# Streaming the high and low parts of an activation in one 512-column matmul, in a two-block transformer kernel

## The chip, the cores and the metric

The kernel runs on one core of a Trainium2 chip. The metric is the device time of one execution in microseconds (us); less is better. The time before is the median of three runs.

## The reference

Two transformer layers are computed one after the other in float32 on x of 256 tokens by 2048 features. Nearly all the arithmetic is in products with large weights:

```python
# first block
u = rms_norm(x); hq, hf, hi, hg, aq, ak, av = split(u @ w_in)        # 2048 x 7168
h = x + rms_norm(concat(hgrn2(hq, hf, hi, hg), dilated_attn(aq, ak, av)) @ w_out)
up = conv3(rms_norm(h) @ w_up); gate, val = split(up)                # 2048 x 11264
h = h + rms_norm((gelu(gate) * val) @ w_down)                        # 5632 x 2048
h = h + (p @ w_pe) * sigmoid(h @ w_pg)
# second block
q, k, v, u, vg = split(rms_norm(h) @ w_in_2)                         # 2048 x 5120
h = h + concat(diff_attn(q, k, v), gmlp(gelu(u), gelu(vg))) @ w_out_2
f = rms_norm(h)
h = h + (silu(f @ w1_2) * (f @ w3_2)) @ w2_2                         # 2048 x 11264, 5632 x 2048
h = h + (p_2 @ pl_w_up_2) * sigmoid(h @ pl_w_gate_2)
out = rms_norm(h)
```

## The kernel before

Every product with a weight is computed as three products of reduced-precision parts. An operand `a` is split into a high part (a cast to the type fp32r) and a low part (`a` less its high part), and `w*a` becomes `whi*ahi + whi*alo + wlo*ahi`.

The weights are streamed in **units** of 512 KB (256 rows of the contraction by 512 columns, 128 partitions of 4 KB): `load` (line 148) issues the transfer on SP's queue into one of three `raw` buffers, `split` (line 155) makes the high part on ScalarE (line 163) and the low part on VectorE (line 164), each with four buffers. `run` (line 166) walks through all 856 units in the order in which the phases have listed them: it issues the load of unit i+5, the split of unit i+3, the matmuls of unit i, then the unit's `post` if it is the last of its group, and then one `tick`. A tick advances each of the side tasks (generators) by one piece; norms, attention heads and evictions are such tasks. So the order of instructions on every engine is written out here, in units, and engines work through their queues in order.

`group` (line 194) lists the units of one **group**, 512 output columns. It accumulates in one tile of PSUM of 1024 columns (two banks), and there are two such tiles. Form "A" has the activation stationary and 512 columns of the weight moving. Form "B" (lines 231 to 243) has a 128x128 piece of the weight stationary and 256 tokens moving: per unit 4 column blocks x 2 contraction tiles x 3 matmuls,

```python
for q, (w_, m_) in enumerate(((hi, ah), (hi, al), (lo, ah))):
    self.mm(ps[:, n * T:(n + 1) * T], w_[:, b, n * P:(n + 1) * P], m_, s, lst and b == 1 and q == 2)
```

With `first` the contraction tile is the outer loop, so that a group can start before all its tiles are there. All matmuls come from line 192.

After a group's last unit its epilogue evicts PSUM: `scaled` (line 279) multiplies each bank by the reciprocal norm on VectorE (line 282); `gate_ep` (line 952) takes a sigmoid on ScalarE; `post_norm` (line 763) squares on ScalarE and scales on VectorE; `residual_ep` (line 1247) adds to h on VectorE (line 1252). High and low parts of the activations are in separate tiles `bh`, `bl` (lines 117 and 118; two pairs) and `hid` (line 880), and are made by `part_hi` (ScalarE, lines 294 and 296) and `part_lo` (VectorE, lines 300 and 302).

After a product whose norm is added to h, `post_finish` (line 793) makes the tiles for the next product pair by pair: multiply on POOL (line 809), add on VectorE (line 813), high part, low part, in a pipeline of 11 stages of which the later ones are issued one per tick (line 821). The next product's units are issued between them. What follows needs the new norm only at its eviction: w_up's first epilogue waits for the flag "r3" (line 893), w_in_2's first for "r6" (line 1001), ffn's first for "r8" (line 1300).

Of the 856 units, 776 are of form B and 80 (parts of w_in and w_in_2) of form A. Groups 0 and 1 of w_out and w_out_2 visit their contraction tiles out of order; the last group of pl_w_gate_2 (line 207) is done in three pieces.

Of the kernel before, what the change touches and what calls it, by code (L numbers as in the profile page):

```python
# [16 lines left out]
P = 128  # L17
T = 256
# [9 lines left out]
# columns of the per-feature constants, [128, n] each  # L28
# [15 lines left out]
class Unit:  # L44
    """512 KB of a weight: 256 rows of the contraction by 512 columns."""
# [5 lines left out]
class Kernel:  # L51
# [55 lines left out]
    def setup(self):  # L107
# [27 lines left out]
    def side(self, name, n=512, count=1):  # L135
        """Banks for side products, once as many have been read: done() tells so."""
# [57 lines left out]
    def group(self, name, w, g, form, acts, kus, epilogue, first=None, part=(True, True), hold=None, tail=None):  # L194
        """Units of one group of 512 columns; acts() gives per kt the (hi, lo) moving or stationary operand.
        epilogue(ps) is called, as a task, after the last of them."""
# [3 lines left out]
        def mk(j, ku):  # L200
            def pe(hi, lo):
# [5 lines left out]
                if tail:  # L207
                    # three pieces one after the other over the last two units
# [7 lines left out]
                    for i, (piece, ns) in enumerate(zip(st["pc"], ((0, 1), (2,), (3,)))):  # L216
                        if j == nk - 2 and i:
                            break
                        for ku_, hi_, lo_ in kept if i and late else kept[-1:]:
                            for q_, n in enumerate(ns):  # L220
                                for b in range(2):
                                    ah, al = acts(2 * ku_ + b)
# [6 lines left out]
                    if j < nk - 2:  # L229
                        kept.clear()  # L230
                elif form == "B":
# [4 lines left out]
                    for n, b in order:  # L236
                        ah, al = acts(2 * ku + b)
# [6 lines left out]
                else:  # L244
# [4 lines left out]
                    for t, b in order:  # L249
                        ah, al = acts(2 * ku + b)  # L250
# [19 lines left out]
    def rstd(self, ss, n, name, out=None):  # L270
        """1/sqrt(ss/D + eps) of sums of squares in PSUM."""
# [7 lines left out]
    def scaled(self, ps, dst, rbc, nb=2):  # L279
        """dst[:, 4, T] = ps * rbc, bank by bank."""  # L280
# [24 lines left out]
    def pair_stages(self, out, gain):  # L305
        """hi and lo of two tiles of h (times a gain), apart."""
# [15 lines left out]
    def start(self):  # L322
# [5 lines left out]
        # matmuls on nothing open the tensor engine's clock gate while the first loads are on their way  # L328
# [28 lines left out]
    def first(self, c, go=False):  # L357
        """Chunk c of x: its load, then its two parts and its squares."""
# [8 lines left out]
        bh, bl = self.buf[0]  # L367
# [425 lines left out]
    def post_finish(self, name, sqs, out, gain, nxt):  # L793
# [23 lines left out]
        for s in range(11):  # L817
# [3 lines left out]
            if s > 4 or s % 2:  # L821
                yield 0
# [705 lines left out]
```

## Time and profile before

| | |
|---|---|
| Median of three runs | 2604.04 us (2603.99 to 2606.28) |
| Span of the profiled execution | 2603.7 us |
| TensorE busy | 2574.3 us, 20346 matmuls and as many weight loads |
| VectorE busy | 1546.5 us |
| ScalarE busy | 1191.4 us |
| POOL (GpSimd) busy | 370.9 us |
| Mean granted TensorE clock | 0.995 of full speed |
| DMA | 469.22 MB, mean 180 GB/s |

The profiled execution's own time is its span of 2603.7 us from first to last instruction; the runs' times are 0.3 us above it. Matmuls are pipelined and the profile models their ends, so the time of one is read from the distance between starts. PE is TensorE, PEld its weight loads, DVE VectorE, ACT ScalarE, POOL GpSimd and SP the engine whose queue issues transfers.

### The profile page before, as it was taken

What the parts mean: (1) busy time and instruction counts of PE and PEld (TensorE: products, weight loads), DVE (VectorE), ACT (ScalarE), POOL (GpSimd) and SP (SyncE); (2) the same over time, 40 slices, a digit from 0 to 9 for tenths busy, and PEclk for the clock granted to TensorE, in tenths of its full rate; (3) what the DMA queues carried; (4) which work ended last, traced back from release to release, by engine and by line L of the source; (5) the groups of instructions that cost most, each with busy time, mean ns of one, the idle gap of its engine ahead of it and who ended that gap; (6) DMA issues with size and microseconds to landing.
All of it is one profiled execution on the core that took longest, in us unless ns stands there. A gap on an engine that the chain in (4) does not pass through costs nothing.

```text
span 2603.7 us, 48034 instructions
## 1 busy us (share of the span) xinstructions
PE 2574.3 (99%) x20346; PEld 2523.0 (97%) x20346; DVE 1546.5 (59%) x1619; ACT 1191.4 (46%) x1497; POOL 370.9 (14%) x299
## 2 busy tenths in 40 slices
PE   8999999999999999999999999999999999999998
PEld 7999999999999999999999899999999999999998
DVE  7568885677666666444565575565555555444445
ACT  5554544465544455333455444444444344333344
POOL 5214442220000000000221030010000000000012
PEclk9999999999999999999999999999999999999999
DMA  6554335555555555555555544455555555555554
GB/s 231 190 171 138 131 129 199 181 185 194 183 183 186 181 184 184 185 186 180 193 191 173 202 170 170 161 180 186 181 184 179 187 186 181 184 183 182 186 205 144
DMA packets 129817, 469.22 MB, mean 180 GB/s; under 512 B 14528, under 2 KB 15824, under 8 KB 129344
## 3 DMA queue, kind: packets, MB, share of 16 engines
q1 hardware_dynamic: 127488, 457.17, 51.4%
q0 software_dynamic: 1968, 8.96, 1.0%
q8 instruction: 159, 2.61, 0.4%
q14 instruction: 58, 0.48, 0.1%
q10 hardware_dynamic: 144, 0.01, 0.0%
HBM read 461.10 MB, written 4.98 MB: 179 GB/s over the span
## 4 chain that ended last, share of the span: by engine, by line
PE 97%; DVE 1%; issue 0%; DMA 0%; ACT 0%; DVEq 0%; SPq 0%; ACTq 0%
PE ps_w_in L192 20%; PE ps_w_up L192 20%; PE ps_ffn L192 19%; PE ps_w L192 10%; PE ps_w_down L192 10%; PE ps_w_out L192 7%; PE ps_w_pg L192 4%; PE ps_pl_gate L192 3%; PE sc L192 1%; PE d L192 1%; DVE wlo L164 1%; PE tl L192 0%; DVE bl L302 0%; DMA raw<-w_in 0%; DVE h L813 0%
## 5 line engine op out<-in xcount | busy, mean ns | idle before, releaser
L164 DVE TENSOR_TENSOR wlo<-raw,whi 128x1024 fp32r<-128x1024 f32 x856 | 1119.7, 1311 | 970.8 <-ACT whi L163 967.9
L163 ACT CAST whi<-raw 128x1024 fp32r<-128x1024 f32 x856 | 893.2, 1046 | 1031.3 <-PE ps_ffn L192 220.1
L192 PE MATMUL ps_w_up<-bl,whi 128*128 128x256 f32 x1408 | 400.3, 284 | 3.5 <-DVE bl L302 3.5
L192 PE MATMUL ps_w_up<-bh,whi 128*128 128x256 f32 x1408 | 400.2, 284 | 0.0
L192 PE MATMUL ps_w_up<-bh,wlo 128*128 128x256 f32 x1408 | 400.1, 284 | 0.0
L192 PE MATMUL ps_ffn<-bh,whi 128*128 128x256 f32 x1408 | 399.1, 283 | 0.0
L192 PE MATMUL ps_ffn<-bl,whi 128*128 128x256 f32 x1408 | 399.0, 283 | 0.0
L192 PE MATMUL ps_ffn<-bh,wlo 128*128 128x256 f32 x1408 | 399.0, 283 | 0.0
L192 PEld LDWEIGHTS ps_w_up<-bl,whi 128*128 128x128 f32 x1408 | 271.8, 193 | 3.7 <-DVE bl L302 3.7
L192 PEld LDWEIGHTS ps_w_up<-bh,whi 128*128 128x128 f32 x1408 | 271.8, 193 | 0.0
L192 PEld LDWEIGHTS ps_w_up<-bh,wlo 128*128 128x128 f32 x1408 | 271.8, 193 | 0.0
L192 PEld LDWEIGHTS ps_ffn<-bl,whi 128*128 128x128 f32 x1408 | 270.6, 192 | 0.0
L192 PEld LDWEIGHTS ps_ffn<-bh,whi 128*128 128x128 f32 x1408 | 270.6, 192 | 0.0
L192 PEld LDWEIGHTS ps_ffn<-bh,wlo 128*128 128x128 f32 x1408 | 270.6, 192 | 0.0
L192 PE MATMUL ps_w_in<-bh,whi 128*128 128x256 f32 x896 | 256.8, 287 | 0.0
L192 PE MATMUL ps_w_in<-bh,wlo 128*128 128x256 f32 x896 | 253.9, 283 | 1.1 <-DVE wlo L164 1.1
L192 PE MATMUL ps_w_in<-bl,whi 128*128 128x256 f32 x896 | 253.7, 283 | 0.0
L192 PEld LDWEIGHTS ps_w_in<-bh,wlo 128*128 128x128 f32 x896 | 171.8, 192 | 1.5 <-DVE wlo L164 1.5
L192 PEld LDWEIGHTS ps_w_in<-bh,whi 128*128 128x128 f32 x896 | 171.8, 192 | 0.7 <-ACT whi L163 0.2
L192 PEld LDWEIGHTS ps_w_in<-bl,whi 128*128 128x128 f32 x896 | 171.9, 192 | 0.5
L192 PE MATMUL ps_w_out<-bh,wlo 128*128 128x256 f32 x512 | 145.1, 283 | 1.4 <-DVE wlo L164 1.4
L192 PE MATMUL ps_w_out<-bh,whi 128*128 128x256 f32 x512 | 146.1, 285 | 0.0
(330 smaller groups left out, 5281.0 us busy)
## 6 DMA issues: line engine op xcount, KB each, us to landing
raw<-ffn_w SPq DMA_DIRECT2D x264, 512.0 KB, 4.3
raw<-w_in SPq DMA_DIRECT2D x192, 512.0 KB, 3.3
raw<-w_up SPq DMA_DIRECT2D x176, 512.0 KB, 3.3
raw<-w_down SPq DMA_DIRECT2D x88, 512.0 KB, 3.3
raw<-w_out SPq DMA_DIRECT2D x64, 512.0 KB, 3.3
raw<-w_pg SPq DMA_DIRECT2D x32, 512.0 KB, 3.4
raw<-pl_w_gate SPq DMA_DIRECT2D x32, 512.0 KB, 4.4
x<-xT SPq DMA_DIRECT2D x8, 256.0 KB, 4.4
```

Of the source, the lines that this page charges most:

```text
L163: nc.scalar.copy(out=hf, in_=u.raw)
L164: nc.vector.tensor_tensor(out=lf, in0=u.raw, in1=hf.bitcast(F32), op=ALU.subtract)
L192: self.nc.tensor.matmul(out, lhsT, rhs, start=start, stop=stop, skip_group_check=True)
```

## The change

A new form "C" takes the place of form B for w_up, ffn_w13_2, w_down, ffn_w2_2, w_pg, for the parts of w_in and w_in_2 that were of form B, for columns 1024 and up of w_out and w_out_2, and for columns up to 1536 of pl_w_gate_2. The high and low part of a contraction tile lie side by side in one tile, so that both are 512 neighbouring columns. A unit is still 512 KB, but of 512 rows of the contraction by 256 columns, and a group has 256 output columns. The high part of the weight streams both parts of the activation in one matmul of 512 columns into one bank of PSUM; the low part streams the high part of the activation into the second half of that bank. At the eviction the two halves are added.

```diff
-            h = self.bp.tile([P, KT, T], F32R, name=f"bh{i}", tag=f"bh{i}")
-            l = self.bp.tile([P, KT, T], F32R, name=f"bl{i}", tag=f"bl{i}")
-            self.buf.append((h, l))
+            t = self.bp.tile([P, KT, 2, T], F32R, name=f"bhl{i}", tag=f"bhl{i}")
+            self.buf.append((t[:, :, 0, :], t[:, :, 1, :], t))
...
+                elif form == "C":
+                    hi, lo = (x.rearrange("p a b -> p (a b)").rearrange("p (b n) -> p b n", b=4) for x in (hi, lo))
+                    order = [(n, b) for n in range(2) for b in range(4)]
+                    if first:
+                        order = [(n, b) for b in range(4) for n in range(2)]
+                    for n, b in order:
+                        ah, _, both = acts(4 * ku + b)
+                        cs = slice(n * P, (n + 1) * P)
+                        self.mm(ps[:, n * 512:(n + 1) * 512], hi[:, b, cs], both.rearrange("p a t -> p (a t)"),
+                                fst and b == 0, False)
+                        self.mm(ps[:, n * 512 + T:(n + 1) * 512], lo[:, b, cs], ah, False, lst and b == 3)
...
+    def parts(self, ps):
+        v = ps.rearrange("p (n x t) -> p n x t", n=2, x=2)
+        return v[:, :, 0, :], v[:, :, 1, :]
+
+    def join(self, ps, dst):
+        x, y = self.parts(ps)
+        self.nc.scalar.copy(out=dst, in_=y)
+        self.nc.vector.tensor_tensor(out=dst, in0=x, in1=dst, op=ALU.add)
+        return dst
+
+    def scaled2(self, ps, dst, rbc):
+        self.scale2(self.join(ps, dst), dst, rbc)
+
+    def scale2(self, t, dst, rbc):
+        self.nc.vector.tensor_tensor(out=dst, in0=t, in1=rbc.unsqueeze(1).to_broadcast([P, 2, T]), op=ALU.mult)
```

The epilogues of C groups use these. `post_norm` joins into y, squares that on ScalarE and scales it in place; `gate_ep` joins, then takes the sigmoid; `residual_ep` adds both halves to h one after the other:

```diff
+            if half is not None:
+                k = 4 * g + 2 * half
+                for v in self.parts(ps):
+                    self.nc.vector.tensor_tensor(out=self.h[:, k:k + 2, :], in0=v, in1=self.h[:, k:k + 2, :],
+                                                 op=ALU.add)
```

In `post_finish` the stages are issued at a closer spacing, and w_up's and ffn's epilogues empty PSUM before they wait for the norm; for that the tiles that they write (`z`) are made earlier, with two memsets on POOL in `enter2`:

```diff
-            if s > 4 or s % 2:
+            if s % 2 or s == 10:
                 yield 0
...
-                if j == 0:
-                    yield from self.until("r3")
+                if j > 1:
+                    yield from self.until(f"cv{j - 2}")
+                z = self.z[j % 2]
+                d = z[:, 2 * half:2 * half + 2, 2:]
+                self.join(ps, d)
+                yield from self.until("r3")
+                if j == 0 and half == 0:
                     self.new_hid("hid", 1)
...
+                self.scale2(d, d, self.rbc)
+                if not half:
+                    return
```

In w_in_2 the first epilogue still waits for "r6" before it reads PSUM. The host lays the weights out for the new units.

## Rows read from the trace of the kernel before

**Rows 1.** The page: span, and TensorE's busy time, share and instructions.

```profile
span 2603.7 us, 48034 instructions
PE 2574.3 (99%) x20346; PEld 2523.0 (97%) x20346; DVE 1546.5 (59%) x1619; ACT 1191.4 (46%) x1497; POOL 370.9 (14%) x299
```

**Rows 2.** The page: the chain that ended last, shares of the span by line.

```profile
PE ps_w_in L192 20%; PE ps_w_up L192 20%; PE ps_ffn L192 19%; PE ps_w L192 10%; PE ps_w_down L192 10%; PE ps_w_out L192 7%; PE ps_w_pg L192 4%; PE ps_pl_gate L192 3%; PE sc L192 1%; PE d L192 1%; DVE wlo L164 1%; PE tl L192 0%; DVE bl L302 0%; DMA raw<-w_in 0%; DVE h L813 0%
```

**Rows 3.** TensorE's waits, longest first: us in total, times, longest us.

```profile
PE ps_w_pg L192 <- DVE bl L300: 3.7, 1, 3.7
```

**Rows 4.** The chain in order of time: start us, us, what, matmuls.

```profile
180.64 2.72 PE ps_w_in L192 x12
...
553.36 472.30 PE ps_w_up L192 x3936
```

**Rows 5.** Groups by form, VectorE and ScalarE: busy us, mean ns | idle before.

```profile
L164 DVE TENSOR_TENSOR wlo<-raw,whi 128x1024 fp32r<-128x1024 f32 x856 | 1119.7, 1311 | 970.8 <-ACT whi L163 967.9 <-PE ps_w_in L192 1.2
...
L282 DVE TENSOR_TENSOR z<-ps_w_up,rbc 128x512 f32<-128x512 f32 x44 | 28.3, 686 | 13.9 <-PE ps_w_up L192 13.9
...
L163 ACT CAST whi<-raw 128x1024 fp32r<-128x1024 f32 x856 | 893.2, 1046 | 1031.3 <-PE ps_ffn L192 220.1 <-PE ps_w L192 145.9 <-PE ps_w_down L192 141.2
...
L861 ACT COPY plu<-ps_pl_up 128x512 f32<-128x512 f32 x8 | 4.3, 588 | 1.9 <-PE ps_pl_up L192 1.9
```

**Rows 6.** Stretches: busy us of each engine, granted clock, DMA share, GB/s.

```profile
170.00:400.00 230.00, 228.96 (x1559) 211.73 (x1559) 187.73 (x224) 104.01 (x178) 98.45 (x83) 1.00 0.40 138
...
560.00:1025.00 465.00, 465.00 (x3877) 465.00 (x3876) 319.30 (x389) 235.50 (x288) 28.19 (x21) 1.00 0.53 184
```

**Rows 7.** ScalarE's waits: us in total, times, longest us.

```profile
ACT whi L163 <- PE ps_ffn L192: 220.1, 127, 1.8
...
ACT whi L163 <- DMA raw<-w_in: 56.7, 33, 5.1
```

**Rows 8.** Transfers of w_up: KB each, median us from issue to landing.

```profile
raw<-w_up SPq DMA_DIRECT2D x176, 512.0 KB, 3.3
```

**Rows 9.** Timeline of VectorE at w_up's beginning: start us, us, instructions.

```profile
519.39 0.87 DVE L302 SCALAR_TENSOR_TENSOR bl<-h,cst,bh 128x256 fp32r<-128x256 f32 x2
...
520.79 0.87 DVE L302 SCALAR_TENSOR_TENSOR bl<-h,cst,bh 128x256 fp32r<-128x256 f32 x2
521.58 1.21 DVE L164 TENSOR_TENSOR wlo<-raw,whi 128x1024 fp32r<-128x1024 f32 x1
...
523.32 0.87 DVE L302 SCALAR_TENSOR_TENSOR bl<-h,cst,bh 128x256 fp32r<-128x256 f32 x2
```

**Rows 10.** The chain in order of time, beginnings of w_up and w_pg.

```profile
515.29 37.21 PE ps_w_up L192 x287
...
1297.03 31.40 PE ps_w_pg L192 x239
```

**Rows 11.** Timeline of VectorE at w_pg's beginning.

```profile
1300.80 0.68 DVE L300 TENSOR_TENSOR bl<-h,bh 128x512 fp32r<-128x512 f32 x1
...
1302.00 0.68 DVE L300 TENSOR_TENSOR bl<-h,bh 128x512 fp32r<-128x512 f32 x1
```

**Rows 12.** Timeline of ScalarE in w_in_2: first and last of the statistics' eight instructions.

```profile
1415.56 1.28 ACT L275 ACT_TABLE_LOAD   x1
...
1421.95 0.20 ACT L276 ACTIVATE rcol<-rcol 128x2 f32<-128x2 f32 x1
```

**Rows 13.** TensorE's waits from 1390 to 1440 us.

```profile
PE ps_w_in L192 <- DVE wlo L164: 1.1, 2, 0.8
```

**Rows 14.** Timeline of TensorE at w_up's beginning.

```profile
515.29 0.58 PE L192 MATMUL ps_w_up<-bl,whi 128*128 128x256 f32 x1 [3.46 <-DVE bl L302]
...
516.10 0.42 PE L192 MATMUL ps_w_up<-bl,whi 128*128 128x256 f32 x1
516.31 0.41 PE L192 MATMUL ps_w_up<-bh,wlo 128*128 128x256 f32 x1
...
521.00 0.29 PE L192 MATMUL ps_w_up<-bh,whi 128*128 128x256 f32 x1
```

More of the change, by code (lines that the diff above doesn't have):

```diff
@@ L366, in first @@
             return
[L367 removed]
+        bh, bl, _ = self.buf[0]
         xc = self.xc.pop(c)
@@ L729, in enter2 @@
         self.ple("p2T")
+        self.zp = self.push("conv", side="right")
+        self.z = []
+        for i in range(2):
+            z = self.zp.tile([P, 4, T + 2], F32, name=f"z{i}", tag=f"z{i}")
+            nc.gpsimd.memset(z[:, :, 0:2], 0.0)
+            self.z.append(z)
     def ple(self, name):
@@ L765, in post_norm, with ep @@
         sqs = []
-        def ep(g):
+        def ep(g, half=None):
             def f(ps):
                 nc = self.nc
-                if g == 0:
+                if g == 0 and not half:
                     self.yp = self.push(f"y{name}", side="right")
@@ L921, in phase3 @@
         for j in range(FT // 2):
-            self.group("w_up", "w_up", j, "B", acts, range(8), ep(j), first=j == 0)
+            for half in range(2):
+                self.group("w_up", "w_up", 2 * j + half, "C", acts, range(4), ep(j, half), first=j + half == 0)
     def phase4(self):
@@ L930, in ep0 @@
             self.ple("pT")
-            return ep(0)(ps)
-        for g in range(4):
-            self.group("w_down", "w_down", g, "B", self.hid, range(FT // 2), ep(g) if g else ep0)
+            return ep(0, 0)(ps)
+        for g in range(8):
+            self.group("w_down", "w_down", g, "C", self.hid, range(FT // 4), ep(g // 2, g % 2) if g else ep0)
         def ep_pe(g):
@@ L964, in gate_ep @@
         for f in stages:
-            for b in range(2):
-                f(2 * g + b)
+            f(g)
             yield 0
@@ L1245, in diff_head, with residual_ep @@
         self.flags.update((f"mixb{2 * h}", f"mixb{2 * h + 1}"))
-    def residual_ep(self, g, out, gain, flag):
+    def residual_ep(self, g, out, gain, flag, half=None):
         def f(ps):
+            if half is not None:
+                k = 4 * g + 2 * half
+                for v in self.parts(ps):
+                    self.nc.vector.tensor_tensor(out=self.h[:, k:k + 2, :], in0=v, in1=self.h[:, k:k + 2, :],
+                                                 op=ALU.add)
+                for s in (*self.pair_stages(out, gain), *((self.sq_stage,) if flag else ())):
+                    s(2 * g + half)
+                yield 0
+                if g == 3 and half and flag:
+                    yield from self.rest(2)
+                    yield from self.stats(flag)
+                return
             for b in range(2):
@@ L1279, in ep0 @@
             self.pop("p6a")
+            self.zp = self.push("glu", side="right")
+            self.z = {}
             self.new_acc("acc7")
@@ L1309, in f @@
                 self.hid_pair(j, z[:, 0:2, :])
+                self.flags.add(f"gl{j}")
             return f
         for j in range(FT // 2):
-            self.group("ffn", "ffn_w13_2", j, "B", acts, range(8), ep(j))
+            for half in range(2):
+                self.group("ffn", "ffn_w13_2", 2 * j + half, "C", acts, range(4), ep(j, half))
     def phase9(self):
@@ L1354, in ep @@
             return f
-        for g in range(4):
-            self.group("pl_gate", "pl_w_gate_2", g, "B", acts, range(8), ep(g),
-                       tail=self.last_piece if g == 3 else None)
+        for g in range(6):
+            self.group("pl_gatec", "pl_w_gate_2c", g, "C", acts, range(4), ep(g))
+        self.group("pl_gate", "pl_w_gate_2", 0, "B", acts, range(8), ep(6), tail=self.last_piece)
     def last_piece(self, i, ps):
```

263 lines of the change are left out of this document (154 added, 109 removed).

## Prediction

> **What bounds the kernel now.** I read the page first: TensorE is busy for 2574.3 us of a span of 2603.7 us [rows 1], and the chain that ended last is made of matmuls of line 192, weight by weight, with nothing else over 1% [rows 2]. So time comes off only where TensorE issues less, or where it stops waiting. It waits little: its longest stop between units is 3.7 us [rows 3]. That leaves the price of a matmul. Durations of single matmuls overlap, so the pitch is read from the chain in order of time: 3936 matmuls of 256 columns took 472.30 us, 120.0 ns each; 12 matmuls of 512 columns (the form in which the weight is the moving operand) took 2.72 us, 226.7 ns each [rows 4]. 512 columns cost 13.3 ns less than twice 256 columns: a matmul has a fixed part of about that size, and the change removes fixed parts.
>
> **What it removes.** In a unit of form B each of the 8 (column block, contraction tile) pairs issues three 256-column matmuls: 24 x 120.0 ns = 2.880 us. In form C the first two become one of 512 columns: 8 x (226.7 + 120.0) = 2.773 us. Form C takes 352 units of w_up and ffn_w13_2 (88 groups of 4), 176 of w_down and ffn_w2_2 (16 groups of 11), 64 of w_in, 48 of w_in_2, 32 of the two w_out, 32 of w_pg and 24 of pl_w_gate_2: 728 of 856, in 154 groups. So 5824 matmuls go, and as many weight loads: 5824 x 13.3 ns = **77.7 us**. The 80 units of form A and the 48 left in form B stay as they are. No row shows a 512-column matmul right after a 256-column one. Its bounds are 226.7 ns and 240.0 ns, twice the short one [rows 4]. I take 226.7: that row has the same width, type and engine, and at a pitch of 120 ns a weight load of the same size already hides beneath each short matmul, so it does beneath a long one.
>
> The Trainium skill ("TensorE: Matmul & The Clock Gate", section Back-to-back issue gap) gives the gap as the columns at 2.4 GHz plus 2.5 ns. By it a fused pair would save 2.5 ns and the whole change 14.6 us; the rows show a fixed part five times as long and decide here, but the rule returns among the rivals.
>
> **What it adds beside TensorE.** The halves of a C group lie side by side in PSUM, so each group gets one ScalarE copy of 128x512 (588 ns by the row of plu) and one more VectorE pass over 512 columns (686 ns by the row of z) [rows 5]; a residual gets a second add and no copy. In w_up VectorE is busy for 319.30 us of 465 and ScalarE for 235.50 [rows 6]: 7.9 and 5.8 us per four units. With 0.69 and 0.59 more that is 8.6 and 6.4 of 11.09 us. It fits, and I cost it at nothing. VectorE's add waits for the copy, the copy for the group's last matmul, and the next split of a weight is queued behind both; TensorE wants that split three units later. The cover is this lead: with four buffers ScalarE casts unit i+3 once unit i-1 has left TensorE, and it does wait for just that, 127 times in ffn alone [rows 7]. Cast and subtraction take 1.05 + 1.31 us [rows 5] and some gaps, so a low part is ready some 5 us ahead; the group's extra 1.3 us eats a quarter of it. Without the cover every group would show its 1.3 us: 154 x 1.3 = 200 us. The densest stretch is 170 to 400 us, with VectorE busy for 187.73 of 230 us [rows 6]; the eight C groups there add 5.5 us, and up to 0.8 us each of waiting for the copy: 201 of 227 us. Zero; bound 2 us. A PSUM buffer is freed about 1.5 us after its group ends and wanted again after 11.09 us. Two memsets move ahead on POOL's queue to where nothing of TensorE's hangs on them: zero. Weights stay 512 KB per unit, one transfer each on SP's queue, landing after 3.3 us [rows 8]; the pace rises by 4%: zero.
>
> **What it moves: the borders.** Four C units run through all 16 contraction tiles in 11 us where eight B units took 23. After a norm these tiles are just being made, so TensorE catches up with VectorE.
> *Border 1, norm to w_up.* TensorE starts at 515.29 [rows 10]; VectorE ends the next pairs of tiles at 520.26, 521.66 and 524.19 [rows 9]. Unit 0 now needs two pairs: it runs half, waits from 517.9 to 519.9 and ends at 522.4; unit 1 needs the fourth pair and ends at 525.6. The fifth pair, the next split (its cast waits for the end of unit 0), pairs six and seven, one more split and the last pair follow on VectorE by the durations of [rows 9]: 525.7, 526.9, 528.4, 529.2, 530.4, 531.3. Unit 3 can end at about 532.8. Before, 288 matmuls ended at 515.29 + 37.21 = 552.50 [rows 10], so unit 3 ended at 552.50 - 8 x 2.88 = 529.5. Worse by 3.3, and 0.4 counted above isn't gained: **3.8 us**.
> *Border 2, norm to w_pg*, in the same way, with pairs done at 1301.48 and 1302.68 and 0.6 us per step after [rows 11]: unit 3 ends at 1312.9 against 1297.03 + 31.40 - 6 x 2.88 = 1311.2 [rows 10]: **2.2 us** with the 0.4.
> *Border 3, w_pg to w_in_2.* The first group's eviction waits until the statistics are issued, after unit 6, but the group now ends with unit 3 and holds its PSUM buffer. Group 2 wants it at 8 x 2.773 + 1.7 (sums on TensorE) = 23.9 us after w_pg's end. The statistics end on TensorE at 18.3; ScalarE then needs 6.6 us, four table loads among it (1415.56 to 1422.15 [rows 12]), then copy and add 1.4: 26.3. A stop of 2.5 us, and 0.8 at a late split after it; 1.1 was lost there before [rows 13]. **2.2 us** more.
> *Clock.* After the stop of 3.46 us the pitch was 213 ns, the lower level, until 521.0 [rows 14]. The borders now have several stops in a row, so the lower level may last longer: from nothing to (all four units at it) 4.9 and 6.5 us. I take **3 us**, nearer the lower end since TensorE is mostly busy between the stops.
> *Thin leads.* At w_in_2's beginning and in pl_gate other transfers share the way, and casts wait for w_in's weights 33 times [rows 7]; some of the gain isn't realised: 0 to 4, I take **2 us**.
>
> **Sum.** -77.7 + 3.8 + 2.2 + 2.2 + 3 + 2 = -64.5 us: 2603.7 becomes 2539.2. The runs' median is 2604.04, 0.3 above the span; so I forecast **2540 us**, 2.5% less.
>
> **The rivals.**
> *The borders cost nothing*, since splits or table loads fall otherwise: 2604.0 - 77.7 = 2526. For it: each loss is a small difference of worked-out times. Against it: the pairs of rows 9 can't come earlier. Chance 0.1.
> *The borders cost double or more*, 27 to 45 us: the lower clock through all four units at two borders (11.4 us), 2 us in the dense stretch, and a stop like border 3's at the other evictions that wait for a flag (w_up, ffn). 2553 to 2571, most likely 2556. For it: the clock did fall after one stop. Against it: in w_up and ffn the new code drains PSUM before it waits. Chance 0.12.
> *The fused matmul saves too little*, and nothing changes. As a mechanism of this kernel: the 13.3 ns of rows 4 would belong to which operand moves and not to the number of matmuls, and the fused one would take almost what two took, 237.7 ns: 240 - 13.2 us of border losses / 5824. Time 2604. Against it: the two forms of rows 4 load and stream the same sizes. Chance 0.03. The skill's rule above would put the change here, its 14.6 us against 13.2 lost.
> *The fused matmul saves nothing*, and the change is slower. Its place is every one of the 5824; at 240 ns they take what two took, while the borders' 13.2 us stay: 2617. It decides from the same 237.7 ns upwards. For it only that no row shows the two widths alternating; against it rows 4. Chance 0.02.
> *It doesn't do what it says*, two loads of the high part staying: they would hide beneath a longer matmul, and no other time comes of it.
>
> **How the numbers follow.** The forecast has 0.73, within about 2532 to 2552 (losses of 6 to 26 us). A measurement of this kernel can tell about 0.2%, 5 us. Faster: 0.73 + 0.1 + 0.12 = 0.95; within 0.2%: 0.03; slower: 0.02. The range for 8 in 10 goes from the rival without losses, 2526, to losses of some 30 us, 2556.
>
> **What would show it.** In the profile after: matmuls of 512 and 256 columns in turn, with pitches of 226.7 and 120 ns, eight of each per unit; stretches of one weight at 2.77 us a unit (w_up 488 us, w_down 244 us); 14522 matmul records in place of 20346. TensorE waiting for low parts of lines 302 and 300 more than once at the first two borders, and for a PSUM buffer early in w_in_2; a low granted clock for 6 to 10 us at each. VectorE near 78% in w_up, its split still waiting for ScalarE. The forecast is wrong if the fused matmul's pitch is above 230 ns, if a C group waits for its PSUM buffer in the steady stretches, or if w_up takes over 495 us.

## The result, and the profile after

The changed kernel takes 2579.5 us (median of four runs, 2565.4 to 2582.7), the kernel before 2604.1: a ratio of 0.9893, 95% interval 0.9869 to 0.9918, so 1.1% less. I had forecast 2540 and a range of 2526 to 2556. The sign is right, the size is not: the saving is 25 us in place of 64. The profiled run took 2578.1 us, its span is 2576.4.

The page of the changed kernel, its span, the engines' busy times and two of the costliest groups (busy us, mean ns of one):

```profile
span 2576.4 us, 36608 instructions
PE 2532.7 (98%) x14522; PEld 2208.0 (86%) x14522; DVE 1626.5 (63%) x1780; ACT 1255.4 (49%) x1639; POOL 407.7 (16%) x299
...
L191 PE MATMUL ps_w_up<-bhl,whi 128*128 128x512 f32 x1408 | 501.0, 401 | 5.7 <-DVE bhl L330 3.7
...
L191 PE MATMUL ps_w_up<-bhl,wlo 128*128 128x256 f32 x1408 | 396.7, 282 | 0.0
```

5824 matmuls are gone, as counted: 14522 in place of 20346 [rows 1]. Busy time doesn't give their price, since their ends overlap (401 + 282 ns stand in a group row, where two starts are 353 ns apart). That comes from the chain in order of time (start us, us, what, matmuls):

```profile
97.15 55.52 PE ps_w_inc L191 x319
...
548.95 469.22 PE ps_w_up L191 x2656
1018.17 248.75 PE ps_w_down L191 x1408
...
1733.51 489.01 PE ps_ffn L191 x2768
2222.52 248.75 PE ps_w L191 x1408
```

In w_up 2656 matmuls, 1328 pairs of a long (512 columns) and a short one (256), took 469.22 us: **353.3 ns a pair**. In a part of w_in 319 took 55.52 us, 348 ns a pair including small stops; where no stop lies between, single starts there are 346.7 ns a pair apart, my forecast's 226.7 + 120.0. So one kernel has two prices for the same pair. I call them the 347 and the 353 rhythm; a unit of eight pairs takes 2773 or 2827 ns, before it was 2880 [rows 4]. The timeline of TensorE in a stretch of the 353 rhythm (start us first) shows it in single starts:

```profile
1413.70 0.40 PE L191 MATMUL ps_w_in_2c<-bhl,whi 128*128 128x512 f32 x1
1413.94 0.28 PE L191 MATMUL ps_w_in_2c<-bhl,wlo 128*128 128x256 f32 x1
1414.06 0.40 PE L191 MATMUL ps_w_in_2c<-bhl,whi 128*128 128x512 f32 x1
1414.30 0.28 PE L191 MATMUL ps_w_in_2c<-bhl,wlo 128*128 128x256 f32 x1
1414.41 0.40 PE L191 MATMUL ps_w_in_2c<-bhl,whi 128*128 128x512 f32 x1
1414.64 0.28 PE L191 MATMUL ps_w_in_2c<-bhl,wlo 128*128 128x256 f32 x1
1414.76 0.40 PE L191 MATMUL ps_w_in_2c<-bhl,whi 128*128 128x512 f32 x1
```

The short one follows the long one after 0.24, 0.24 and 0.23 us and the next long one comes 0.11 to 0.12 us later; the pattern repeats every three pairs, 1.06 us.

TensorE's waits (us in total, times, longest us), for [rows 3, 13]:

```profile
...
PE ps_w_pg L191 <- DVE bhl L328: 3.9, 1, 3.9
PE ps_w_up L191 <- DVE bhl L330: 3.7, 1, 3.7
PE ps_w_in_2c L191 <- DVE gu L306: 2.9, 1, 2.9
...
PE ps_w_in_2c L191 <- DVE bhl L330: 2.0, 1, 2.0
PE ps_w_up L191 <- ACT bhl L324: 1.9, 2, 1.7
PE ps_w_pg L191 <- ACT bhl L322: 1.6, 1, 1.6
```

The stops before w_pg and w_up are those of before. New are the second waits at w_up and w_pg (1.9 and 1.6), in w_in_2 a wait for a low part of the activation (2.0) and one for a PSUM buffer (`gu`, line 306, is the eviction's add), and two in the attention (matmuls `o` and `d`; their lines are shown with e6).

Where the 27.3 us between the two spans (2603.7 and 2576.4) come from is seen by laying the traces on each other. The 856 units are in the same order, so I take the start of each unit's last matmul with the weight's low part in both and subtract: the time saved up to that unit. This is worked out from the traces' starts, no view of the profile:

```
up to unit                              us saved   step
 47  end of w_in's first C groups          4.37
111  end of w_in                          0.67     -3.70
147  last before w_up                     1.52     +0.85
163  w_up's sixteenth                    -1.04     -2.56
415  last before w_pg                    12.19    +13.23
419  w_pg's fourth                        9.74     -2.45
447  last of w_pg                        12.61     +2.87
463  w_in_2's sixteenth                  10.20     -2.41
557  last but two of w_out_2             12.74     +2.54
565  ffn's sixth                         12.32     -0.42
847  end                                 27.36    +15.04
```

In the long steady stretches the saving grows by 0.053 us a unit, half of the 0.107 that I forecast. At the borders and in the attention it falls. The beginning differs between executions: up to unit 47 two more profiles of this same program (e13 and e14 below) saved 4.31 and 1.55 us. So below the steps are compared and not the sums.

### The profile page after: what moved, and what is told of

Read it like the earlier page. It is cut to its first block, busy times and chain, and to the rows that moved or that the text cites. A ratio compares the mean times of both kernels' runs of the same rounds, so it can differ in the third digit from the quotient of the medians.

```text
span 2576.4 us, 36608 instructions
## 1 busy us (share of the span) xinstructions
PE 2532.7 (98%) x14522; PEld 2208.0 (86%) x14522; DVE 1626.5 (63%) x1780; ACT 1255.4 (49%) x1639; POOL 407.7 (16%) x299
## 4 chain that ended last, share of the span: by engine, by line
PE 91%; DVE 5%; ACT 2%; issue 1%; DMA 1%; POOL 0%; SPq 0%; DVEq 0%; ACTq 0%
PE ps_ffn L191 19%; PE ps_w_up L191 19%; PE ps_w_down L191 10%; PE ps_w L191 10%; PE ps_w_in L191 7%; PE ps_w_inc L191 6%; PE ps_w_in_2c L191 4%; PE ps_w_out L191 3%; PE ps_pl_gatec L191 3%; DVE wlo L163 2%; PE ps_w_pg L191 2%; PE ps_w_outc L191 2%; PE ps_w_out_2c L191 1%; PE sc L191 1%; ACT whi L162 1%
## 5 line engine op out<-in xcount | busy, mean ns | idle before, releaser
L191 PE MATMUL ps_w_up<-bhl,whi 128*128 128x512 f32 x1408 | 501.0, 401 | 5.7 <-DVE bhl L330 3.7
L191 PE MATMUL ps_ffn<-bhl,whi 128*128 128x512 f32 x1408 | 497.8, 399 | 0.0
L191 PE MATMUL ps_w_up<-bhl,wlo 128*128 128x256 f32 x1408 | 396.7, 282 | 0.0
L191 PE MATMUL ps_ffn<-bhl,wlo 128*128 128x256 f32 x1408 | 395.4, 281 | 0.0
L191 PEld LDWEIGHTS ps_w_up<-bhl,whi 128*128 128x128 f32 x1408 | 265.9, 189 | 73.4 <-issue 6.5
L191 PEld LDWEIGHTS ps_ffn<-bhl,whi 128*128 128x128 f32 x1408 | 264.6, 188 | 66.0
L191 PEld LDWEIGHTS ps_w_up<-bhl,wlo 128*128 128x128 f32 x1408 | 267.4, 190 | 0.0
L191 PEld LDWEIGHTS ps_ffn<-bhl,wlo 128*128 128x128 f32 x1408 | 266.0, 189 | 0.0
L191 PE MATMUL ps_w_in<-whi,bhl 128*128 128x512 f32 x640 | 200.9, 395 | 0.0
L191 PE MATMUL ps_w_inc<-bhl,whi 128*128 128x512 f32 x512 | 182.4, 398 | 0.0
```

The source lines that it names most:

```text
L191: self.nc.tensor.matmul(out, lhsT, rhs, start=start, stop=stop, skip_group_check=True)
```

## The experiments

Saved times below are worked out in the same way. A kernel for which no ratio is given ran once. The theories on the pitch that the first expectations speak of: (1) each change of width costs something; (2) the traffic beside TensorE (transfers, splits) slows it; (3) the bank of PSUM does, since the short matmul adds into the bank into which the long one has just written; (4) alternation has two steady rhythms, of which one is taken up after each stop.

**Order and banks.** Three kernels change only the order of the sixteen matmuls of a unit of form C (in the diffs `long` and `short` stand for the two matmuls). The first groups of w_up and w_pg keep the alternation in all three.

```diff
# e1: two long, two short; e2 with order (all eight) for order[i:i + 2]; e5 with four
-                    for n, b in order:
-                        long(n, b); short(n, b)
+                    for r in [order[i:i + 2] for i in range(0, 8, 2)]:
+                        for n, b in r: long(n, b)
+                        for n, b in r: short(n, b)
# e3: alternating, each short one in the other bank than the long one before it
+                    seq = [(n, b) for b in range(4) for n in range(2)]
+                    long(*seq[0])
+                    for x, y in zip(seq[1:], seq): long(*x); short(*y)
+                    short(*seq[-1])
```

Expected of e1 (two and two):

> In a unit of form C the matmuls go two long, two short, in place of one and one (groups with contraction-outer order are left as they are). Theory 1, changes of width: the 353.3 ns that a long and a short matmul take in most of the changed kernel, in place of 346.7, come from each change between 512 and 256 columns; with half the changes the mean per pair is about 350 ns and the kernel gains some 17 us, to about 2560. Theory 2, traffic: the loss comes from what ScalarE, VectorE and the transfers read and write in SBUF meanwhile; order changes nothing, 353 ns stay. Theory 3, bank: the short matmul adds to the half of the bank that the long one has just written; here a long one on the other bank lies between, so the pitch is 346.7 and the kernel gains some 35 us. Theory 4, two steady rhythms: each stop leaves TensorE in one of two rhythms, whatever the order; 346.7 in some stretches and 353.3 in others.

Of e2 (eight and eight):

> In a unit of form C all eight long matmuls go first, then the eight short ones. Theory 1, changes of width: one change back and forth per unit; 8 x 226.7 + 8 x 120.0 = 2.77 us a unit nearly everywhere, 35 to 39 us less than the changed kernel, about 2541. Theory 2, traffic: 2.83 us a unit stay in the long stretches. Theory 3, bank: as theory 1. Theory 4, two rhythms: with a mean pitch of equal widths no second rhythm, as in the kernel before; the same number as theory 1, but pairs2 then shows both rhythms.

Of e3 (other bank):

> Long and short matmuls still alternate, but each short one goes to the other bank than the long one before it (but for the last of a unit). Theory 3, bank: pitch 346.7 in the long stretches, some 35 us less than the changed kernel. Theories 1 and 2: 353.3 stays, no change in time beyond a few us. Theory 4: 353.3 or 346.7 by stretch, as in the changed kernel.

Measured: e1 2555.5 us, ratio 0.9815 [0.9801, 0.983]; e2 2559.3, 0.983 [0.9813, 0.9846]; e3 2579.2, 0.9904 [0.9889, 0.9919]. Their chains, one fence each, w_up and w2, to be laid beside 469.22 and 248.75:

```profile
549.26 462.59 PE ps_w_up L191 x2656
...
2203.68 245.22 PE ps_w L191 x1408
```

```profile
549.39 463.70 PE ps_w_up L191 x2656
...
2207.18 245.81 PE ps_w L191 x1408
```

```profile
555.54 468.08 PE ps_w_up L191 x2656
...
2224.81 248.16 PE ps_w L191 x1408
```

Divided by 166 units that is 2786.7, 2793.3 and 2820 ns a unit, in each of these three kernels the same in every long stretch. Other banks change almost nothing: theory 3 falls. Two and two is better than the change by 0.8%, and the intervals don't touch. But eight and eight, with the fewest changes of width, isn't the best, so a fixed price per change (theory 1) falls too. In e2's trace the eight short ones run at 120 ns, while the long ones behind them start 235, 235, 229, 232, 230, 228 and 226 ns apart: the long one has its 226.7 only after several of its kind.

**Traffic.** e4 leaves out loads and splits of weights in stretches of w_up and ffn and uses older weights again, so its product is another one.

```diff
+        for a, b, k in ((180, 220, 0), (220, 260, 3), (260, 300, 5), (600, 640, 6), (640, 680, 0)):
...
-        self.nc.sync.dma_start(out=u.raw, in_=u.src)
+        if self.kind(i) & 1: self.nc.sync.dma_start(out=self.kraw, in_=u.src)
...
+        if k & 2:
             nc.scalar.copy(out=self.khi.rearrange("p a b -> p (a b)"), in_=u.raw)
+        if k & 4:
             nc.vector.tensor_tensor(out=self.klo.rearrange("p a b -> p (a b)"), in0=u.raw,
```

> Leaves out part of the weights' loading and splitting in five stretches, where older weights are used again (the product is another there): units 180 to 219 nothing is loaded or split, 220 to 259 no low part is made on VectorE, 260 to 299 no high part on ScalarE, 600 to 639 no transfer, 640 to 679 nothing again. Theory 2, traffic: the pair of matmuls falls to 346.7 ns in the two empty stretches and in those without the engine at fault. Theories 1, 3 and 4: 353.3 ns throughout, with the traffic or without.

Measured: 2568.2 us. The chain of e4:

```profile
553.23 460.38 PE ps_w_up L203 x2656
1013.60 244.05 PE ps_w_down L203 x1408
...
1723.82 489.01 PE ps_ffn L203 x2768
```

w_up and w_down ran in the 347 rhythm from beginning to end (460.38 / 166 = 2773 ns a unit), in the units left as they were too; ffn and w2 (248.75 us) in the 353 rhythm, also where nothing was loaded or split. Traffic isn't it: theory 2 falls. It also shows what the rhythm is worth: 8.84 us in w_up and 4.7 in w_down for the same matmuls.

**Four and four, and the attention's evictions.** e6 evicts the attention's q and k with a single pass over the first half of PSUM: it leaves out the copy and the adding of the second half, and so the terms with the low parts.

```diff
-                self.scaled2(ps, z[:, 2 * s:2 * s + 2, :], self.rbc)
+                self.scale2(self.parts(ps)[0], z[:, 2 * s:2 * s + 2, :], self.rbc)
```

> Four long matmuls and then four short ones, instead of two and two (2786.7 ns a unit) or eight and eight (2793.3). If what is lost against 2773.3 ns is paid at each change of width, this order, with two changes to long per unit against four and one, pays less than two and two: under 2780 ns a unit, some 2550 us in all. If the loss belongs to the particular order and not to the count of changes, it lies at 2787 to 2793 or apart from both, 2555 to 2560 us or more. It is also a candidate for the best order.

Measured: 2568.4 us, ratio 0.986 [0.9845, 0.9875], 2806.7 ns a unit in every long stretch, worse than two and two and than eight and eight. The price belongs to the particular order; no count of changes gives it. The chain of e5:

```profile
549.97 465.90 PE ps_w_up L191 x2656
```

> The groups of the attention's q and k evict with one VectorE pass over the first half of PSUM: the copy of the second half and its adding are left out, so these products lack the terms that sat there. Theory: the 5.4 us that the stretch of units 47 to 111 (170 to 400 us) loses against the slow rhythm come from the added eviction work on VectorE and ScalarE; then the loss shrinks to under 2.5 us, and the whole run is 3 us shorter than the changed kernel, if the long stretches keep the same rhythm. Rival: the loss is in the pace of TensorE itself or in waits for other work of that stretch (gates, recurrences), and stays between 4 and 6 us.

Measured: 2570.9 us, 0.9879 [0.9844, 0.9914]. The total can't be compared, since w_up and w_down had the 347 rhythm in the profiled run. From unit 47 to 111 the saved time goes from 1.18 to 1.33 us, +0.15, where the change lost 3.70. TensorE's waits from 150 to 410 us, first of the changed kernel, then of e6:

```profile
PE o L191 <- POOL s L658: 2.6, 2, 1.4
PE d L191 <- DVE ll L328: 1.5, 1, 1.5
PE d L191 <- ACT e L615: 0.7, 1, 0.7
...
```

```profile
PE o L191 <- POOL s L658: 1.6, 2, 1.2
PE apt L735 <- ACT sxs L674: 0.4, 1, 0.4
PE ao L191 <- DVE bhl L328: 0.2, 1, 0.2
PE d L191 <- DVE ll L328: 0.2, 1, 0.2
```

The 32 C units there would save 1.7 us in the 353 rhythm, so the change lost 5.4 and e6 1.6: the added evictions of q and k cost some 3.8 us. In the 16 other profiles of the changed kernel and its variants this step is -3.35 to -3.97 us, so e6's +0.15 is far outside their spread. In TensorE's waits 2.8 of the 3.8 us are seen (5.2 us in all, 2.4 in e6). That they come by way of VectorE's queue, in which the heads' own steps (`ll`, and what feeds `s`) stand behind the evictions, is read from who ends the waits and not tested: e6 takes the copy from ScalarE and the add from VectorE together.

**Stops.** Twelve units get a stop within them: VectorE copies a piece of the weight's low (e7) or high part (e8) to where an earlier matmul of the unit has just read another, so that TensorE waits and goes on with a short or with a long matmul.

```diff
+        self.locks = [160, 200, 240, 280, 320, 360, 400, 570, 610, 650, 690, 720]
...
+                        if lock and k == 0:      # after the first short one; e8: the same with hi, before it
+                            self.nc.vector.tensor_copy(out=lo[:, 0, 0:P], in_=lo[:, 3, P:2 * P].bitcast(F32))
```

> In twelve units (the first fit one from units 160, 200, 240, 280, 320, 360, 400, 570, 610, 650, 690 and 720) the low part that the second short matmul loads is copied by VectorE to where the first one's lay, so that TensorE stops once, by 0.3 to 1 us, and goes on with a short matmul. Theory of two rhythms (the one after a stop is set by what TensorE resumes with, and a short one gives the fast rhythm): 2773.3 ns a unit behind each of the twelve, against 2826.7; w_up, w_down, ffn and w2 then take 25 us less than in the profile of the changed kernel, and the twelve stops give back 4 to 12 us: 2555 to 2568 us, with little spread between runs. Rival (which rhythm follows a stop is chance): of twelve stops some are followed by 2826.7, and the time lies between 2560 and 2590.

> The same twelve stops, but with the high part moved, so that TensorE goes on with a long matmul. Theory of two rhythms with the short one as the cause of the fast rhythm: behind at least half of the twelve stops the slow rhythm, 2826.7 ns a unit, 2575 to 2595 us. Rival (any stop can give either, by chance or by its length): the same mixture as with stops before a short one; or the fast rhythm behind all of them, which would put the cause on the stop alone.

Measured: 2622.2 us, ratio 1.0079 [1.0053, 1.0106], and 2628.3. The stops were far longer than meant. TensorE's waits in e7:

```profile
PE ps_w_up L193 <- DVE wlo L251: 24.8, 5, 5.2
PE ps_ffn L193 <- DVE wlo L251: 12.9, 5, 4.0
...
PE ps_w_down L193 <- DVE wlo L251: 4.4, 2, 2.3
```

The copy itself took 0.22 us, but it stands in VectorE's queue behind all that was issued earlier: 3.5 us a stop, 42 in all. The rhythm is read between stops. Behind those with a short matmul 8 stretches of 12 have 2773 ns a unit, behind those with a long one 9 of 12 (the other seven 2826 to 2827). So what TensorE resumes with doesn't decide; the theory with the short one as cause falls, and the mixture of the rivals stands. In one kernel, e7, two neighbouring stretches of w_up:

```profile
684.24 111.20 PE ps_w_up L193 x621
803.72 109.16 PE ps_w_up L193 x621
```

The same number of matmuls, 621, takes 111.20 us behind one stop and 109.16 behind the next.

**The borders.** e9 and e11 undo the long matmul in the first group of w_up and of w_pg; e10 repeats e1 beside them.

```diff
+                        if first:                        # e9
+                            m256(n, b, hi, 0, 0, fst and b == 0)
+                            m256(n, b, hi, 1, 1, False)
+                        else:
+                            long(n, b)
                         short(n, b)
# e11, on e1: the second of these one contraction tile later
```

> Only in the first group of w_up and of w_pg (four units each) the 512-column matmul is undone: high part times high activation, high part times low activation and low part times high activation as three 256-column matmuls, as in the kernel before. Theory (borders: the long matmul waits for the low half of the activation, which the 256-column one of before did not need): between the units before and behind the border of w_up 2.5 to 3.4 us come back, at w_pg 1.8 to 2.6 us, nothing at w_in. Rival (the borders' loss comes from the later eviction of the group before, or from the weights' splitting that it delays): under 0.8 us comes back at each.

> The order of two long and two short matmuls once more, as the reference for the next one on this chip: 2786.7 ns a unit, 2553 to 2559 us.

> Two long and two short matmuls, and in the first group of w_up and of w_pg three 256-column matmuls, of which those that need the activation's low half come one block of 128 rows later. If the borders' loss is the wait for the low half, 4 to 7 us less than the order of pairs alone: 2549 to 2552 us. If it is not, 2554 to 2557.

Measured: e9 2577.6 us; from unit 147 to 163 it loses 2.41 us (the change 2.56), from 415 to 419 1.94 (2.45). 0.2 and 0.5 us come back, within the rival's 0.8. But the other two profiles of the changed program lose 2.57 and 2.23, 3.35 and 2.07 there, so neither is clear of the spread. And in e9 the low half is still wanted by the second matmul of each pair. So e9 shows that undoing the long matmul alone doesn't bring the loss back, not that the low half is without effect.

e10 took 2559.1, at the upper end. e11 took 2554.5, 0.981 [0.9793, 0.9826], which can't be told from e1; it loses 1.44 us at w_up and 0.78 at w_pg where e1 lost 2.29 and 2.07 (e10 2.10 and 2.08), under 2.2 us together and not the 4 to 7 expected. So the wait for the low half is a part of the loss.

The point with the least spread is the end of w_up's first group, unit 151. From unit 147 to there the three profiles of the changed program lose 3.20, 3.19 and 3.17 us, e1 and e10 3.40 and 3.18, e9 3.05 and e11 2.05.

**A change of order without a stop.**

```diff
+                    if self.cur % 8 == 0 and not first:
+                        long(*order[0]); long(*order[1]); short(*order[0]); short(*order[1])
+                        order = order[2:]
```

> Strict alternation as in the change, but once in every eighth unit two long matmuls and then two short ones, with no stop. If such a change of order draws the rhythm anew, and the fast one comes out as often as behind the stops (9 and 9 of 12), each stretch is a mixture with a mean near 2790 ns a unit, 2555 to 2562 us. If the fast rhythm, once there, outlasts it and only the slow one is left by it, all long stretches are at about 2775 ns a unit after a few of them: 2545 to 2550 us. If a rhythm is changed by a stop alone, the time stays that of the change, 2565 to 2583, with stretches of one rhythm from stop to stop.

(The first of the two counts quoted there should be 8.) Measured: 2580.9 us, 0.9913 [0.9898, 0.9928], with 2826 ns a unit from w_up's twenty-first unit to the end of w_down and from 1780 us through ffn, w2 and pl_gate. The total is that of the third case, but its mechanism isn't what the trace shows: the rhythm does change without a stop. A changed place in ffn, with no wait before any of its matmuls (`x2` are the two long and the two short ones):

```profile
1755.70 0.40 PE L192 MATMUL ps_ffn<-bhl,whi 128*128 128x512 f32 x1
...
1756.76 0.40 PE L192 MATMUL ps_ffn<-bhl,whi 128*128 128x512 f32 x1
...
1757.11 0.63 PE L192 MATMUL ps_ffn<-bhl,whi 128*128 128x512 f32 x2
1757.58 0.39 PE L192 MATMUL ps_ffn<-bhl,wlo 128*128 128x256 f32 x2
1757.81 0.40 PE L192 MATMUL ps_ffn<-bhl,whi 128*128 128x512 f32 x1
...
1758.85 0.39 PE L192 MATMUL ps_ffn<-bhl,whi 128*128 128x512 f32 x1
```

Three pairs take 1.06 us ahead of it and 1.04 behind it. I went through all 78 changed places that lie in unbroken alternation (worked out from starts, no view). In the 353 rhythm a long matmul is followed after 233, 241 and 236 ns in turn. Where the first of the two long ones stood at the step of 236, the 353 rhythm stayed, 66 times of 66; where it stood at one of the other two steps, the 347 rhythm followed, 5 times of 5. From the 347 rhythm 6 of 7 changed places led into the 353. So here the step of the pattern decides. That the long stretches keep to one rhythm follows from the spacing: eight units have 64 pairs, of which 62 alternate, and 62 is twenty patterns of three and two pairs more, so each changed place meets the step of 236 again. Another spacing wasn't tried.

**The same program again, and two groups taking turns.** e13 and e14 are the changed kernel without an edit. e15 starts from e1:

```diff
+    def weave(self):                     # after the first two groups of w_up and of w_pg
+        u = self.units
+        u[-8:] = [u[i] for k in range(4) for i in (k - 8, k - 4)]
```

> The changed kernel as it is, profiled again. If the rhythm is drawn in each execution, at least one of the long stretches (w_up and w_down; ffn, w2 and pl_gate) of this and the next profile has 2773.3 ns a unit where the first profile had 2826.0, and the time is 13 to 17 us shorter for each that has; if the program decides it, both stretches have 2826.0 in both profiles and the times are 2576 to 2583 us.

> The same program a third time. Drawn in each execution: 2773.3 ns a unit in at least one long stretch of this or the profile before it; decided by the program: 2826.0 in both stretches again.

> Two long and two short matmuls, and in w_up and in w_pg the units of the first two groups take turns, so that a contraction tile is wanted every 1.4 us as in the kernel before, not every 0.7. If the borders' loss is this pace, against the order of pairs alone 2 to 3.5 us come back at w_up (by unit 163) and 1 to 2.5 us at w_pg (by unit 430): 2550 to 2553 us. Rival (the loss is made by what precedes the first unit, the longer eviction and the later norm): under 0.7 us at each, 2555 to 2558 us.

Measured: 2580.5 and 2580.2 us, with 2827 ns a unit in both long stretches of both, as if the program decided. The chain of e13:

```profile
549.25 469.22 PE ps_w_up L191 x2656
```

But shorter stretches differ between the three profiles of this one program: behind the first stops of w_up (some 45 pairs from 530 or 533 us) the 353 rhythm twice and the 347 once, at w_in_2's first C groups (from 1412 to 1415 us) the same, in w_pg's beginning the 347 once and the 353 twice. So the program alone doesn't fix the rhythm; the six long stretches of these three profiles all have the 353 one. It needs no stop to change it: at about 550 us four matmuls of a sum of squares stand between two pairs, with no wait, and there e14 goes from the 347 to the 353 rhythm, and e4 from the 353 to the 347. What decides at a stop or at such a place stays open.

e15 took 2558.9 us, 0.9822 [0.9806, 0.9839]. It loses 2.16 us from unit 147 to 163 and 1.95 from 415 to 430, e1 2.29 and 1.15: the pace across units isn't it either. But nearly all of it, 2.34, is lost in w_up's first unit; the next seven lose nothing more in sum (-2.83 behind the first, -2.79 behind the eighth). The timeline of TensorE there, the starts with a wait before them (in brackets):

```profile
515.86 0.77 PE L191 MATMUL ps_w_up<-bhl,whi 128*128 128x512 f32 x1 [3.67 <-DVE bhl L338]
...
520.50 0.76 PE L191 MATMUL ps_w_up<-bhl,whi 128*128 128x512 f32 x1 [1.66 <-ACT bhl L332]
```

**Half units.** So e16 lets each unit of the first group leave its third and fourth tile until the second group's unit has used the first two.

```diff
+                        if j < nk - 1 and first == 1:
+                            self.rest_ = mine[2:]
+                            mine = mine[:2]
+                        elif j < nk - 1:
+                            mine = mine[:2] + self.rest_ + mine[2:]
```

> As with the two groups taking turns, but each unit of the first group leaves its third and fourth contraction tile until the second group's unit has used the first two, so that two tiles serve 2.8 us of matmuls as in the kernel before. If the first loss is made by the four tiles that a unit wants, at least 1.3 us of the 2.6 lost from unit 147 to 149 come back at w_up and 1 us at w_pg (from unit 415 to 419), and the time is 2 to 4 us under that kernel: 2553 to 2557 us. If it is made by what precedes the unit, both stay within 0.5 us.

Measured: 2557.2 us, 0.9817 [0.98, 0.9833]. From unit 147 to 149 0.42 us are lost and not 2.63; from 415 to 419 1.02 are gained where e15 lost 2.71. In the same timeline only the first stop is left:

```profile
516.11 0.77 PE L191 MATMUL ps_w_up<-bhl,whi 128*128 128x512 f32 x1 [3.67 <-DVE bhl L352]
```

Up to unit 151 it loses 0.32 us where e15 lost 2.53 and e1 3.40. All 16 other profiles, with units of 512 rows left whole, lost 1.6 to 3.5 us from unit 147 to 149 and 0.8 to 3.4 from 415 to 419. So the border's loss is made by the 512 rows of a unit: it wants four tiles where two were wanted. At w_up it isn't a gain in the end, because two groups that end together wait for their eviction (unit 156):

```profile
PE ps_w_up L191 <- DVE z L328: 2.5, 1, 2.5
```

What w_pg gave is lost again in w_in_2: from unit 447 to 463 4.81 us go, in e15 3.82, in e10 3.73, in e1 0.72. Why this step varies so much I didn't look into.

The best kernels of the series are the orders of two long and two short, e1 (2555.5) and e11 (2554.5): 1.9% under the kernel before, with 2786.7 ns a unit in the long stretches.

## Why the prediction was wrong, and where it was right

**What bounds it, and the count: right.** TensorE bounds both kernels, and 5824 matmuls went.

**The price of a pair: wrong, and this is the step that failed.** "I take 226.7: that row has the same width, type and engine" prices a long matmul among others of its kind. In the prediction stood the sentence that no row shows one right after a short one, and between the bounds of 226.7 and 240.0 I took one end. Measured as the pair less 120.0, it is 226.7 in one rhythm and 233.3, the middle of the bounds, in the other. All pairs in the 353 rhythm would save 5824 x 6.67 = 38.8 us. In the profile 607 of 5367 undisturbed pairs (judged in windows of six), 11%, had the 347 one, so about 43 us were saved (38.8 and another 6.67 ns for 11% of the pairs) and not 77.7. That is 35 of the 37 us between my 2539.2 and the span. The two signs that I had named for this came: a pitch above 230 ns, and w_up at 504 us (513.9 to 1018.2), above 495. The rivals on this term were too extreme: for "saves too little" 237.7 ns had to hold, and I gave nothing to the ground between.

The rule of the Trainium skill ("TensorE: Matmul & The Clock Gate", section Back-to-back issue gap) that I weighed, 2.5 ns a matmul, is not borne out by either rhythm: a pair saves 6.7 or 13.3 ns. The section states that figure for an isolated matmul, which I had left out.

**The added evictions: right in the steady stretches, wrong in the attention.** In w_up no C group waits for PSUM in the steady part and VectorE is busy for 320.89 of 440 us, 73% (I had said 78). In the attention I took zero with a bound of 2 us; the loss was 5.4 us, of which e6 gave back 3.8. The sum of busy times said that the work fits (I wrote 201 of 227 us, whose own terms give 199.6; measured 192.86 of 230); it doesn't say who waits in a queue. The windows of the changed kernel (busy us of PE, PEld, DVE, ACT, POOL, then granted clock, DMA share, GB/s), for [rows 6], and behind them the second one as e13 had it:

```profile
170.00:400.00 230.00, 224.53 (x1287) 195.09 (x1286) 192.86 (x232) 106.01 (x183) 105.21 (x84) 1.00 0.45 135
512.00:540.00 28.00, 24.14 (x115) 20.04 (x116) 22.65 (x30) 16.88 (x29) 11.53 (x8) 0.82 0.48 160
560.00:1000.00 440.00, 440.00 (x2493) 381.52 (x2492) 320.89 (x414) 243.13 (x316) 42.31 (x20) 1.00 0.60 187
1286.00:1316.00 30.00, 28.41 (x147) 24.32 (x147) 22.80 (x26) 16.23 (x22) 7.51 (x10) 0.87 0.48 151
...
512.00:540.00 28.00, 22.34 (x114) 18.30 (x115) 22.66 (x30) 16.89 (x29) 11.53 (x9) 0.94 0.51 161
```

**The borders: right in place and nearly in size.** Against the 353 rhythm's gain the three borders lose 3.4 (2.56 + 16 x 0.053), 2.7 and 3.3 us, 9.4 together with the clock; I had 3.8, 2.2 and 2.2, and 3 for the clock. In border 1 unit 3 was to lose 3.3 us by the tiles' times; it lost 3.2 (1.52 to -1.68), in the other two profiles of the program 3.19 and 3.17. e16 shows the cause as predicted, the pairs of tiles; the wait for the low half is a part of it, as e11 shows, and not the whole, as the expectations of e9 and e11 had it. The stop for the PSUM buffer in w_in_2 was 2.9 us (2.5 forecast), ended by the eviction's add.

**The clock: longer at the lower level, but hardly paid.** The granted clock is 0.82 over 28 us at w_up, 0.88 in the same window of the kernel before: 28 x 0.06 = 1.7 us of full speed less. The window at w_pg begins when the clock has already been low for some time; in the 20 us behind unit 415 it is 0.74, and 0.83 before: 20 x 0.09 = 1.8 us. But at w_up e13 had a granted clock of 0.94 and lost the same up to unit 151, so there the tiles set the time and not the clock. At w_pg the loss from unit 415 to 419 was 2.07 to 3.35 us in the three profiles of the program, least where the clock was highest (0.91 in the 20 us behind unit 415 in e14, 0.74 in the two others): at most 1.3 us.

**Thin leads: wrong in place.** I had put 2 us to w_in_2's beginning and to pl_gate. In pl_gate nothing is lost: from ffn's sixth unit to the end the saving grows by 0.053 us a unit throughout. About 0.8 us are lost at the end of w_out_2 (-0.42 in place of +0.43), where TensorE waits 0.64 us for a low part of VectorE and for no transfer.

All losses together, 5.4 + 9.4 + 0.8 = 15.6 us, against 13.2 forecast: 43 - 15.6 = 27.4, beside the 27.3 that the spans show. That the losses came near as a sum is in part luck: the attention, put at nothing, lost 5.4, and clock and thin leads less than I had. The gain, taken from one row of twelve matmuls of another form, was nearly twice too large. The 0.3 us that I added between span and run are 1.7 in the run profiled here (2578.1 and 2576.4), which changes nothing.

## What to carry to other kernels

A matmul's price read from a run of equal matmuls holds for that run; where a change mixes widths, take the ground between the bounds as the likeliest case and not one end, and try the order of the matmuls before giving up the gain: two long and two short gave 24 us more here than one and one. Where a unit of work takes in more rows of the contraction, ask at each border how many of its operands exist when it starts. And where busy times say that added work fits, list what is queued behind it on its engine. A difference between two single profiles means something only beside the spread of one program profiled again.

## What the hardware showed that I had not expected

Strictly alternating matmuls of 512 and 256 columns run in one of two steady rhythms, 346.7 and 353.3 ns a pair, that last for hundreds of microseconds as long as nothing breaks the alternation. A stop, four other matmuls in between (550 us in e14 and e4) or a change of order without any wait (e12) can lead from one to the other, and the same program takes different ones in the same stretch from run to run. Neither traffic nor the kind of matmul after a stop decides which. For a change of order the step of the three-pair pattern does: in e12 66 places at one step left the 353 rhythm as it was, and 5 at the other two led into the 347. Once, in e9 at 2505 us, the 353 rhythm went over into the 347 with nothing in between that the trace shows.

The runs of the changed kernel spread over 17 us (2565 to 2583). This fits a long stretch in one rhythm or the other (w_up and w_down in the 347 one take 8.84 + 4.7 us less in e4), but the run of 2565 has no trace; those of e1, e2, e3 and e5 lie within 4 us of their medians. The price of the same sixteen matmuls by order: 2773 or 2827 ns (one and one), 2787 (two and two), 2807 (four and four), 2793 (eight and eight), 2820 (one and one in different banks). What in TensorE makes this was not found; the weight loads (0.19 us each, longer than the 120 ns of a short matmul) were left alone in every run.
